# Layer norm woven between the y units, the last Q units behind the last convolution eviction, both halves of the out-projection behind the last y, the conv bias loaded early

## The chip, the core and the metric

The kernel runs on one core of a Trainium2 chip. The metric is the device time of one execution in microseconds. Five engines work from their own instruction queues, each in its own order: TensorE (PE in the profile, its weight loads PEld), VectorE (DVE), ScalarE (ACT), GpSimd (POOL) and SyncE (SP), which issues nearly all DMAs. An instruction waits for semaphores of other engines or DMAs; everything behind it on its engine waits with it.

## The reference

Two encoder layers on a sequence of 512 with 1024 channels, in f32. The change lies in the first layer's mixer:

```
z = h @ w_in                                   # 512 x 1536: za, zg, u
a = za * sigmoid(zg)
a = depthwise_conv(a, conv_w, width 31) + conv_b
ya = silu(layer_norm(a, ln_g, ln_b))           # 512 channels
y  = s5 forward + s5 backward + d * u          # 32 groups x 16 channels, 64 states
y  = gelu(y)
yb = y * sigmoid(y @ glu_w + glu_b)
h  = concat(ya, yb) @ w_out
x  = x + h
```

Behind it come the first feed-forward (SwiGLU, 2816 wide), the neighbourhood attention of the second layer and its feed-forward.

## The kernel before, in words

The order of the work is written out by hand: each engine does its instructions in the order in which the code emits them. Three things bend this order around the change.

*Background work.* `bgV` holds generators of small VectorE jobs. `tick(ns)` gives credit; jobs are emitted until their estimated costs have used it up, `charge(ns)` takes credit away, and `finish(job)` emits what is left of a job at once. The jobs here are the eight Q units, `job_q[i, hf]` (lines 969 to 977), each three VectorE instructions of 128 x 1024 (line 436: Q, wq, and Q plus wq), which make the operand of the y matmuls. Each of the 16 convolution steps gives `TCONV` of credit.

*Weights.* `W` streams 512 KB chunks: `load` issues the DMA on SyncE (line 73), `split` makes the high part `whi` on ScalarE (line 90) and the rest `wlo` on VectorE (line 92), and then loads the next chunk. `W.ahead()` splits up to two chunks ahead.

*PSUM.* Two rings of four banks, `psa` (convolution, mean, variance, cT, wo) and `psb` (y, yT, glu).

The stage goes like this. The convolution is four banks of four steps; each step is a set of small matmuls (line 993) against Toeplitz tables that ScalarE writes (line 761), one pair of steps' tables by VectorE (line 773). When a bank is full, VectorE adds the conv bias and writes it out (line 1003, into `an`) and sums it for the layer norm (line 1005, `lns`). The bias `cbB` comes by two DMAs on SyncE, behind the loads of the state-space tables `T`.

Then come four y units, `out_y(i, hq)`: each 4 groups of matmuls against T (line 1022) and Q (line 1025), and one eviction on ScalarE into `yn` (line 1028). `out_y(0, 0)` needs the Q units (0,0) and (2,0), `out_y(1, 1)` needs (1,1) and (3,1). The layer norm is in two parts: `ln_mean` (mean over channels by matmul, line 1064; two subtractions on VectorE, line 1068; eight squares with sums on ScalarE, line 1072) and `ln_scale` (variance by matmul, line 1077; a reciprocal root in twelve small VectorE instructions; scaling, line 1083 on VectorE, line 1081 on ScalarE). `out_a(ct)` transposes the normed rows back (cT, line 1090), applies silu (line 1102) and splits the result into `mah` and `mal`. `out_half(p, ...)` is one half of the out-projection of this branch: 24 matmuls of 128 x 512 (lines 200 to 202, tile `wo`). `out_t(ct)` transposes y (yT, line 1090; copy at line 1037), of which ct 0 and 2 need only the first two y units; `gelu` follows on both vector engines (lines 1043 to 1053) and then the GLU matmuls.

Of the kernel before, what the change touches and what calls it, by code (L numbers as in the profile page):

```python
# [19 lines left out]

CAP = 3000.0
HV = (4, 4)
TCONV = 2200
TCV = 10
QN, QT = 0, 2
LN, LT, LV = 1, 4, 6
# [4 lines left out]
P = 128  # L31
# [84 lines left out]
def tile_hybrid_encoder(ctx, tc, x, mix_norm, ffn_norm, ffn_w_gate, ffn_w_up, ffn_w_down,  # L116
# [4 lines left out]
    nc = tc.nc  # L121
# [48 lines left out]
    W = Weights(nc, wp, seq, NIN)  # L170
# [3 lines left out]
    def psa(name="psa"):  # L174
        return psp.tile([P, 512], F32, tag="a", name=name, bufs=4)

    def psb(name="psb"):
        return psp.tile([P, 512], F32, tag="b", name=name, bufs=4)
# [17 lines left out]
    def tmp(shape, tag, bufs=2, dt=F32):  # L196
        return sm.tile(shape, dt, tag=tag, name=tag, bufs=bufs)
# [76 lines left out]
    class Background:  # L274
# [20 lines left out]
        def tick(self, ns):  # L295
            self.credit = min(self.credit, CAP) + ns * self.share
            while self.credit > 0 and (self.jobs or self.fill):
                if self.jobs:
                    self.step()
                else:  # L300
                    self.step_fill()
# [16 lines left out]
    bgV = Background(1.0)  # L318
# [334 lines left out]
    for i in range(4):  # L653
# [19 lines left out]
        if i == 1:  # L673
# [4 lines left out]
            for t in range(4):  # L678
# [4 lines left out]
                         in_=ps[:, 64:64 + 4 * TAPS].rearrange("p (t j) -> p t j", t=4), func=AF.Copy)  # L683
# [3 lines left out]
            for t in range(LCH):  # L687
                p0 = 64 * (t % 2) + 16 * (t // 2)
                nc.sync.dma_start(out=wv[p0:p0 + 16],
                                  in_=bass.AP(tensor=wdb.tensor, offset=wdb.offset + t,  # L690
                                              ap=[[WPAD, 16], [16 * WPAD, G], [1, NLAG]]))
            A.activation(out=hgb, in_=col[:, R_GB:R_GB + 4], func=AF.Copy, scale=0.5)
        if i == 2:
            for r in range(2):
                ps = psb("ct")
                for t in range(4):
                    PE.transpose(out=ps[:, t * P:(t + 1) * P],
                                 in_=cnat[:, r, t].rearrange("p d n -> p (d n)"), identity=ident)
# [56 lines left out]
    def g_tc(n):  # L755

        t = slots[n // 2 % 3]
        for i in range(2):
            tcs[n + i] = t[:, :, i]
        for c in range(16):  # L760
            A.activation(out=t[:, :, :, c], in_=wvs[:, :, n:n + 2], func=AF.Copy, scale=mask16[:, c:c + 1])
            yield 1

    def make_tc(n):
        if n != TCV:
            for _ in g_tc(n):
                pass
            return
        t = slots[n // 2 % 3]
        for i in range(2):  # L770
            tcs[n + i] = t[:, :, i]
            for h in range(2):
                V.tensor_tensor(out=t[:, h, i], in0=wvs[:, h, n + i].unsqueeze(1).to_broadcast([P, 16, NLAG]),
                                in1=mask16.unsqueeze(2).to_broadcast([P, 16, NLAG]), op=ALU.mult)
        bgV.charge(3300)

    def g_tc_early():
        yield from g_tc(0)
        yield from g_tc(2)
# [51 lines left out]
    def scan_tables(i):  # L831
        e = phase[i]
        A.activation(out=e[:, 0], in_=e[:, 2], func=AF.Copy, scale=-1.0)
        A.activation(out=decays[:, i % 2, :, 1:], in_=m8[:, 1, 4 * i:4 * i + 4].unsqueeze(2).to_broadcast([P, 4, NCH - 1]),
                     func=AF.Copy)
# [59 lines left out]
    make_pb(3)  # L895
    scan_tables(0)
    tc_early = g_tc_early()
    f, b = slice(0, 64), slice(64, 128)
    for q in range(2):
        A.activation(out=pwQ[b, q].rearrange("p g t -> p t g"), in_=pw[b, q, 1:9], func=AF.Copy)  # L900
# [67 lines left out]
    def g_q(i, hf):  # L968
        yield from fused(Q[i][:, hf], wq, pwQ, 2 * i + hf, CT, CTs)


    cbB = tmp([P, 16, 16], "rstdB", 1)
    for h in range(2):
        src = conv_b[0, 256 * h:256 * h + 256]
        nc.sync.dma_start(out=cbB[64 * h:64 * h + 64],
                          in_=bass.AP(tensor=src.tensor, offset=src.offset, ap=[[0, 64], [1, 256]]))
    job_q = {(i, hf): g_q(i, hf) for i, hf in ((0, 0), (2, 0), (0, 1), (2, 1), (1, 0), (3, 0), (1, 1), (3, 1))}
    bgV.fill += job_q.values()
    for _ in tc_early:
# [6 lines left out]
    for b in range(4):  # L986
        ps = psa("conv")
        for gi in range(4):
            n = 4 * b + gi
            t = tcs.pop(n)  # L990
            for l in range(5):
                for h in range(2):
                    PE.matmul(out=ps[64 * h:64 * h + 64, gi * P:gi * P + P],
                              lhsT=AC[:, 16 * h + n, l:l + NCH],
                              rhs=t[:, h, :, 8 * l:8 * l + 8],
                              start=(l == 0), stop=(l == 4))
            if n % 2 and n + 5 < 16:
                make_tc(n + 5)
            tick(TCONV)
        if b == 2:  # L1000
            W.ahead()
        gs = slice(4 * b, 4 * b + 4)
        V.tensor_tensor(out=yc[:, :, gs], in0=ps.rearrange("p (g c t) -> p t g c", g=4, t=LCH),
                        in1=cbB[:, gs].unsqueeze(1).to_broadcast([P, LCH, 4, 16]), op=ALU.add)
        V.tensor_reduce(out=lns[:, b], in_=yc[:, :, gs].rearrange("p t g c -> p t (g c)"), axis=AX.X, op=ALU.add)
        bgV.charge(1200)
# [4 lines left out]
    def out_y(i, hq, between=None):  # L1011
        for key in ((i, hq), (i + 2, hq)):
            if key in job_q:
                bgV.finish(job_q[key])
        ps = psb("y")
        for gi in range(4):
            if gi == 2 and between is not None:
                between()
            gs = [h * 16 + i * 8 + hq * 4 + gi for h in range(2)]
            o = [ps[64 * h:64 * h + 64, gi * P:(gi + 1) * P] for h in range(2)]  # L1020
            for h, g in enumerate(gs):
                PE.matmul(out=o[h], lhsT=U[:, g], rhs=T[:, :, g], start=True, stop=False)
            for r in range(2):
                for h, g in enumerate(gs):
                    PE.matmul(out=o[h], lhsT=S2[:, r, g],
                              rhs=Q[g // 8][:, hq, r, gi].rearrange("p t c -> p (t c)"),
                              start=False, stop=(r == 1))
        A.activation(out=yn[:, :, i * 8 + hq * 4:i * 8 + hq * 4 + 4],
                     in_=ps.rearrange("p (g t c) -> p t g c", g=4, t=LCH), func=AF.Copy)
# [25 lines left out]
    def gelu(*cts):  # L1055
        for _ in g_lockstep(*(g_gelu(ct) for ct in cts)):
            pass
# [3 lines left out]
    def ln_mean():  # L1061
        ps = psa("mean")
        for b in range(4):
            PE.matmul(out=ps[:, 0:LCH], lhsT=pair, rhs=lns[:, b], start=(b == 0), stop=(b == 3))
        yv = yc.rearrange("p t g c -> p t (g c)")
        q = tmp([P, LCH], "lnq", 1)
        for t0 in (0, 4):
            V.tensor_tensor(out=yv[:, t0:t0 + 4], in0=yv[:, t0:t0 + 4],
                            in1=ps[:, t0:t0 + 4].unsqueeze(2).to_broadcast([P, 4, 256]), op=ALU.subtract)
            for t in range(t0, t0 + 4):  # L1070
                d = tmp([P, 256], "diag")
                A.activation(out=d, in_=yv[:, t], func=AF.Square, accum_out=q[:, t:t + 1])
        lnt["q"] = q

    def ln_scale():
        ps = psa("var")
        PE.matmul(out=ps[:, 0:LCH], lhsT=pair, rhs=lnt["q"], start=True, stop=True)
        r = rsqrt(ps[:, 0:LCH], LCH, 1e-5, 1.0)
        for t in range(LCH):
            if t in LNA:  # L1080
                A.activation(out=yc[:, t], in_=yc[:, t], func=AF.Copy, scale=r[:, t:t + 1])
            else:
                V.tensor_scalar(out=yc[:, t], in0=yc[:, t], scalar1=r[:, t:t + 1], scalar2=None, op0=ALU.mult)
# [9 lines left out]
    def mix_tile(n):  # L1093
        return lp.tile([P, 4, S], F32R, tag="Q", name=n, bufs=4)
# [11 lines left out]
    def out_a_low(ct):  # L1106
        V.tensor_tensor(out=mal[:, ct], in0=ya.pop(ct), in1=mah[:, ct].bitcast(F32), op=ALU.subtract)

    out_y(0, 0)
    bgV.finish(job_q[1, 0])  # L1110
    ln_mean()
    out_y(0, 1)
    out_y(1, 0)
    ln_scale()
    mah, mal = mix_tile("mah"), mix_tile("mal")
    for ct in range(4):
        out_a(ct)
    bgV.finish(job_q[1, 1])
    for ct in range(4):
        out_a_low(ct)  # L1120

# [2 lines left out]
    def out_half(p, mh, ml, first, ps_of=None):  # L1124
        wh, wl = W.next()
        W.ahead()
        for mi in range(2):
            m = 2 * p + mi
            if first:
                po[m] = ps_of("wo")  # L1130
            c = slice(mi * P, mi * P + P)
            for k in range(4):
                mm3(po[m], wh[:, k, c], wl[:, k, c], mh[:, k], ml[:, k], first and k == 0,
                    not first and k == 3)

    out_half(0, mah, mal, True, psa)
    out_y(1, 1)
    ygs = mp.tile([P, 2, 4, S], F32R, tag="S2", name="ygs")
    ygh, ygl = ygs[:, 0], ygs[:, 1]
    for ct in (0, 2, 1, 3):  # L1140
        out_t(ct)
    gelu(0, 2)
    gelu(1, 3)
    out_half(1, mah, mal, True, psa)
    mbh, mbl = mix_tile("mbh"), mix_tile("mbl")
# [68 lines left out]
    for m in range(KD):  # L1214
        ps = psa("dn")
        for a, b in ((0, 8), (8, 16), (16, 22)):
            wh, wl = W.next()
            W.ahead()
            for k in range(a, b):
# [20 lines left out]
                                          ap=[[465, 16], [-31, 8], [1, 248]]))  # L1240
# [145 lines left out]
    for n, cg in enumerate(QKV_ORDER):  # L1386
# [5 lines left out]
        for i in range(4):  # L1392
# [13 lines left out]
            for kk in range(2):  # L1406
                k = 2 * i + kk
                for j in range(4):
# [4 lines left out]
                    else:  # L1413
                        a, b = VSP[j - 1]
# [136 lines left out]
```

## Time and profile before

| | us |
|---|---|
| median of 3 runs | 1235.96 |
| runs | 1235.87 to 1237.0 |
| the profiled execution, device time | 1235.37 |
| its span in the trace | 1233.6 |
| TensorE matmul busy | 1198.1 (97%) |
| VectorE busy | 663.5 (54%) |
| ScalarE busy | 476.9 (39%) |
| GpSimd busy | 41.6 (3%) |
| TensorE busy from 150 to 200 us | 34.49 of 50 |

The table says that TensorE works nearly all the time. A share of the whole span hides the one stage that differs, from about 140 to 213 us: the end of the convolution, the y units, the layer norm, the out-projection's first part and the GELU. A timeline row of the section below gives the start, the length from the first instruction's start to the last one's end, the engine, the line of the kernel, the operation, the tiles written and read, the shapes and the count; in square brackets stands how long the engine had been idle before, and what released it. TensorE's clock has two levels, 1.2 and 2.4 GHz; the granted clock is the share of the higher one.

### The profile page before, as it was taken

The numbers are of one execution on the slowest core, as the hardware profiler recorded it, in microseconds if no ns is written. First come the engines' busy times: TensorE is split into PE (matmuls) and PEld (weight loads), VectorE is DVE, ScalarE is ACT, GpSimd is POOL, SyncE is SP. The second block draws the span as 40 slices with busy tenths as digits, with TensorE's granted clock in tenths as the row PEclk, the third lists the DMA queues.
The fourth block names the chain that finished last, engine by engine and source line by source line (L and its number), as shares of the span: only waits on it lengthen the run. The fifth ranks groups of instructions, "written<-read, shape, count | busy, mean of one in ns | idle before, by whom it ended". The sixth has DMA issues, their size and how long they took to land.

```text
span 1233.6 us, 16107 instructions
## 1 busy us (share of the span) xinstructions
PE 1198.1 (97%) x6427; PEld 951.3 (77%) x6427; DVE 663.5 (54%) x1110; ACT 476.9 (39%) x840; POOL 41.6 (3%) x90
## 2 busy tenths in 40 slices
PE   7999778999999999999999999999999999999998
PEld 4655566888888888888888887678888888888886
DVE  8899875664444444333337554856544444452322
ACT  5757756432232332222225465744323233222120
POOL 1100000000000000000000001520000000000000
PEclk9999978999999999999999999999999999999999
DMA  7411510333333323333354443303323333323331
GB/s 158 94 52 52 124 36 18 107 99 99 89 103 103 102 86 95 96 94 94 99 158 128 150 140 90 107 26 102 96 87 102 103 103 88 100 86 103 120 103 34
DMA packets 173154, 118.04 MB, mean 96 GB/s; under 512 B 21193, under 2 KB 153593, under 8 KB 173080
## 3 DMA queue, kind: packets, MB, share of 16 engines
q1 hardware_dynamic: 172616, 115.92, 32.4%
q10 hardware_dynamic: 400, 1.07, 0.4%
q8 instruction: 50, 0.82, 0.3%
q14 instruction: 24, 0.20, 0.0%
q0 software_dynamic: 64, 0.03, 0.0%
HBM read 109.04 MB, written 7.96 MB: 95 GB/s over the span
## 4 chain that ended last, share of the span: by engine, by line
PE 92%; DVE 3%; DMA 2%; SPq 2%; ACT 1%; issue 0%; DVEq 0%; POOL 0%; ACTq 0%; POOLq 0%
PE up L200 6%; PE gate L200 6%; PE gate L202 6%; PE up L202 6%; PE gate L201 6%; PE up L201 6%; PE qkv L1416 4%; PE qkv L1418 4%; PE qkv L1417 4%; PE dn L201 3%; PE dn L202 3%; PE dn L200 3%; PE dn L1517 3%; PE dn L1515 3%; PE dn L1516 3%; PE zg L730 2%
## 5 line engine op out<-in xcount | busy, mean ns | idle before, releaser
L92 DVE TENSOR_TENSOR wlo<-wraw,whi 128x1024 fp32r<-128x1024 f32 x176 | 213.0, 1213 | 256.0 <-ACT whi L90 254.7
L90 ACT ACTIVATE whi<-wraw 128x1024 fp32r<-128x1024 f32 x176 | 183.6, 1045 | 282.2 <-issue 113.9
L200 PE MATMUL gate<-xgh,whi 128*128 128x512 f32 x352 | 137.2, 390 | 0.0
L200 PE MATMUL up<-xgh,whi 128*128 128x512 f32 x352 | 137.1, 390 | 0.0
L202 PE MATMUL gate<-xgh,wlo 128*128 128x512 f32 x352 | 137.0, 389 | 0.0
L202 PE MATMUL up<-xgh,wlo 128*128 128x512 f32 x352 | 137.0, 389 | 0.0
L201 PE MATMUL gate<-xgl,whi 128*128 128x512 f32 x352 | 136.9, 389 | 0.0
L201 PE MATMUL up<-xgl,whi 128*128 128x512 f32 x352 | 136.9, 389 | 0.0
L1200 DVE TENSOR_TENSOR fu<-up,rstdB 128x512 f32<-128x512 f32 x44 | 30.4, 691 | 113.3 <-PE up L202 113.3
L1202 ACT ACTIVATE gh<-fu 128x512 fp32r<-128x512 f32 x44 | 27.8, 632 | 150.7 <-DVE fu L1201 150.7
L202 PEld LDWEIGHTS gate<-xgh,wlo 128*128 128x128 f32 x352 | 66.1, 188 | 13.8
L202 PEld LDWEIGHTS up<-xgh,wlo 128*128 128x128 f32 x352 | 66.0, 188 | 13.9
L201 PEld LDWEIGHTS gate<-xgl,whi 128*128 128x128 f32 x352 | 66.1, 188 | 13.7
L200 PEld LDWEIGHTS up<-xgh,whi 128*128 128x128 f32 x352 | 66.2, 188 | 13.6
L200 PEld LDWEIGHTS gate<-xgh,whi 128*128 128x128 f32 x352 | 66.0, 188 | 13.6
L201 PEld LDWEIGHTS up<-xgl,whi 128*128 128x128 f32 x352 | 66.0, 188 | 13.6
L200 PE MATMUL dn<-gh,whi 128*128 128x512 f32 x176 | 69.3, 394 | 0.0
L201 PE MATMUL dn<-gl,whi 128*128 128x512 f32 x176 | 69.3, 394 | 0.0
L202 PE MATMUL dn<-gh,wlo 128*128 128x512 f32 x176 | 69.3, 394 | 0.0
L1517 PE MATMUL dn<-whi,gl 128*128 128x512 f32 x176 | 69.2, 393 | 0.0
L1515 PE MATMUL dn<-whi,gh 128*128 128x512 f32 x176 | 69.0, 392 | 0.0
L1416 PE MATMUL qkv<-whi,xgh 128*128 128x512 f32 x176 | 68.8, 391 | 0.0
(298 smaller groups left out, 2017.0 us busy)
## 6 DMA issues: line engine op xcount, KB each, us to landing
wraw<-in_ffn_w_gate_dram SPq DMA_DIRECT2D x44, 512.0 KB
wraw<-in_ffn_w_up_dram SPq DMA_DIRECT2D x44, 512.0 KB
wraw<-in_ffn_w_down_dram SPq DMA_DIRECT2D x38, 512.0 KB
wraw<-in_na_w_qkv_dram SPq DMA_DIRECT2D x24, 512.0 KB
wraw<-in_ab_w_in_dram SPq DMA_DIRECT2D x12, 512.0 KB
bt<-bd SPq DMA_DIRECT2D x8, 640.0 KB
wraw<-in_ab_w_out_dram SPq DMA_DIRECT2D x8, 512.0 KB
wraw<-in_na_w_out_dram SPq DMA_DIRECT2D x8, 512.0 KB
```

What stands on the lines that cost most here:

```text
L90: self.nc.scalar.activation(out=hi, in_=raw, func=AF.Copy)
L92: eng.tensor_tensor(out=lo, in0=raw, in1=hi.bitcast(F32), op=ALU.subtract)
L200: PE.matmul(out=o, lhsT=lh, rhs=rh, start=start, stop=False)
L201: PE.matmul(out=o, lhsT=lh, rhs=rl, start=False, stop=False)
L202: PE.matmul(out=o, lhsT=ll, rhs=rh, start=False, stop=stop)
L1200: V.tensor_tensor(out=u, in0=pu, in1=rB, op=ALU.mult)
L1416: PE.matmul(out=pq[j], lhsT=lh, rhs=wh[:, kk], start=(k == 0), stop=False)
L1417: PE.matmul(out=pq[j], lhsT=lh, rhs=wl[:, kk], start=False, stop=False)
L1418: PE.matmul(out=pq[j], lhsT=ll, rhs=wh[:, kk], start=False, stop=(k == 7))
L1515: PE.matmul(out=pd[j], lhsT=gh[:, k, c], rhs=wh[:, kk], start=(k == 0), stop=False)
L1516: PE.matmul(out=pd[j], lhsT=gh[:, k, c], rhs=wl[:, kk], start=False, stop=False)
L1517: PE.matmul(out=pd[j], lhsT=gl[:, k, c], rhs=wh[:, kk], start=False, stop=(k == NF - 1))
```

## The change

`TCONV` goes from 2200 to 1750, so each convolution step emits less of the Q units. The bias DMAs move to the front of the state-space stage and `cbB` takes a buffer of the tag `diag`. `W.ahead()` moves from behind the third convolution bank to behind the layer norm's scaling. `ln_mean` is emitted between the second and third group of the first y unit, `ln_scale` behind the second y unit, `out_y(1, 1)` before the first half of the out-projection, and both halves stand behind the transposes of y, with half of the GELU emitted before each.

```
-TCONV = 2200
+TCONV = 1750
...
     tc_early = g_tc_early()
+    cbB = tmp([P, 16, 16], "diag")
+    for h in range(2):
+        src = conv_b[0, 256 * h:256 * h + 256]
+        nc.sync.dma_start(out=cbB[64 * h:64 * h + 64],
+                          in_=bass.AP(tensor=src.tensor, offset=src.offset, ap=[[0, 64], [1, 256]]))
...
-    cbB = tmp([P, 16, 16], "rstdB", 1)
-    for h in range(2):
-        src = conv_b[0, 256 * h:256 * h + 256]
-        nc.sync.dma_start(out=cbB[64 * h:64 * h + 64],
-                          in_=bass.AP(tensor=src.tensor, offset=src.offset, ap=[[0, 64], [1, 256]]))
...
             tick(TCONV)
-        if b == 2:
-            W.ahead()
...
-    out_y(0, 0)
-    bgV.finish(job_q[1, 0])
-    ln_mean()
+    out_y(0, 0, ln_mean)
+    for key in ((1, 0), (3, 0)):
+        bgV.finish(job_q[key])
     out_y(0, 1)
+    ln_scale()
+    for key in ((1, 1), (3, 1)):
+        bgV.finish(job_q[key])
+    W.ahead()
     out_y(1, 0)
-    ln_scale()
     mah, mal = mix_tile("mah"), mix_tile("mal")
     for ct in range(4):
         out_a(ct)
-    bgV.finish(job_q[1, 1])
+    out_y(1, 1)
     for ct in range(4):
         out_a_low(ct)
...
-    out_half(0, mah, mal, True, psa)
-    out_y(1, 1)
     ygs = mp.tile([P, 2, 4, S], F32R, tag="S2", name="ygs")
     ygh, ygl = ygs[:, 0], ygs[:, 1]
     for ct in (0, 2, 1, 3):
         out_t(ct)
     gelu(0, 2)
+    out_half(0, mah, mal, True, psa)
     gelu(1, 3)
     out_half(1, mah, mal, True, psa)
```

The instructions of every engine are the same in number; only their places differ. VectorE before, from the third bank's eviction to the layer norm (`an<-conv` is the eviction with the bias, `lns` its sum, `wlo` the weight splits, `an<-an,mean` the subtraction):

```order
L436 TENSOR_TENSOR Q<-pwQ,CT 128x1024
L92 TENSOR_TENSOR wlo<-wraw,whi 128x1024 x2
L1003 TENSOR_TENSOR an<-conv,rstdB 128x8x64
L1005 TENSOR_REDUCE lns<-an 128x8
L436 TENSOR_TENSOR wq<-pwQ,CTs 128x1024
L436 TENSOR_TENSOR Q<-Q,wq 128x1024
L1003 TENSOR_TENSOR an<-conv,rstdB 128x8x64
L1005 TENSOR_REDUCE lns<-an 128x8
L1068 TENSOR_TENSOR an<-an,mean 128x1024 x2
```

The same place on VectorE in the changed kernel:

```order
L1001 TENSOR_TENSOR an<-conv,diag 128x8x64
L1003 TENSOR_REDUCE lns<-an 128x8
L436 TENSOR_TENSOR Q<-Q,wq 128x1024
L436 TENSOR_TENSOR Q<-pwQ,CT 128x1024
L436 TENSOR_TENSOR wq<-pwQ,CTs 128x1024
L436 TENSOR_TENSOR Q<-Q,wq 128x1024
L436 TENSOR_TENSOR Q<-pwQ,CT 128x1024
L1001 TENSOR_TENSOR an<-conv,diag 128x8x64
L1003 TENSOR_REDUCE lns<-an 128x8
L1066 TENSOR_TENSOR an<-an,mean 128x1024 x2
```

Before, all Q instructions and two weight splits stand ahead of the last eviction. Now two Q instructions (wq and Q of the last unit) and the splits stand behind the scaling:

```order
L1081 TENSOR_SCALAR an<-an,rs_y 128x256 x5
L436 TENSOR_TENSOR wq<-pwQ,CTs 128x1024
L436 TENSOR_TENSOR Q<-Q,wq 128x1024
L92 TENSOR_TENSOR wlo<-wraw,whi 128x1024 x2
L1105 TENSOR_TENSOR mal<-sq,mah 128x512
```

ScalarE before, behind the convolution's tables (`diag,lnq<-an` are the squares, `yn` the y evictions, `sq<-cT` the first silu):

```order
L90 ACTIVATE whi<-wraw 128x1024 x2
L1028 ACTIVATE yn<-y 128x8x64
L1072 ACTIVATE diag,lnq<-an 128x256 x8
L1028 ACTIVATE yn<-y 128x8x64 x2
L1081 ACTIVATE an<-an,rs_y 128x256 x3
L1102 ACTIVATE sq<-cT,col 128x512
```

The same place on ScalarE in the changed kernel:

```order
L1070 ACTIVATE diag,lnq<-an 128x256 x8
L1026 ACTIVATE yn<-y 128x8x64 x2
L1079 ACTIVATE an<-an,rs_y 128x256 x3
L90 ACTIVATE whi<-wraw 128x1024 x2
L1026 ACTIVATE yn<-y 128x8x64
L1100 ACTIVATE sq<-cT,col 128x512
```

The weight copies move from ahead of the squares to behind the scaling, and the third y eviction behind them. On TensorE the mean stands between the second and third group of the first y unit, the variance between the second and third y unit, and the fourth y unit between the transposes cT and yT; the 24 matmuls of the first `out_half`, which stood right behind cT, stand behind yT.

## Rows read from the trace of the kernel before

**Rows 1.** Stages: busy us by engine (PE, PEld, DVE, ACT, POOL), granted clock, DMA.
```profile
150.00:200.00 50.00, 34.49 (x390) 31.02 (x388) 35.33 (x51) 28.14 (x76) 0.00 (x0) 0.80 0.10 30
```

**Rows 2.** Timeline of PE, 143 to 213 us: start, length, engine, line, tiles, count.
```profile
143.21 4.07 PE L993 MATMUL conv<-tcb,AC 128*64 128x128 f32 x40 [2.51 <-ACT tcb L761]
...
163.64 2.40 PE L993 MATMUL conv<-tca,AC 128*64 128x128 f32 x40 [1.78 <-ACT tca L761]
165.87 0.39 PE L1022 MATMUL y<-T,U 128*64 128x128 f32 x4
...
168.59 0.61 PE L1064 MATMUL mean<-lns,wpad 128*128 128x8 f32 x4
...
176.53 0.60 PE L1064 MATMUL mean<-lns,wpad 128*128 128x8 f32 x2 [3.12 <-DVE lns L1005]
...
184.34 0.39 PE L1077 MATMUL var<-lnq,wpad 128*128 128x8 f32 x2
...
188.80 3.28 PE L1090 MATMUL cT<-ident,an 64*128 64x64 f32 x32 [4.07 <-DVE an L1083]
...
202.40 1.78 PE L1090 MATMUL yT<-ident,yn 64*128 64x64 f32 x32
...
204.11 0.50 PE L200 MATMUL wo<-mah,whi 128*128 128x512 f32 x1
...
209.68 0.39 PE L200 MATMUL glu<-ygs,whi 128*128 128x512 f32 x1
...
212.54 0.50 PE L200 MATMUL glu<-ygs,whi 128*128 128x512 f32 x1 [1.34 <-ACT ygs L1051]
```

**Rows 3.** Timeline of DVE, 134 to 189 us.
```profile
134.30 1.23 DVE L436 TENSOR_TENSOR Q<-pwQ,CT 128x1024 f32<-128x1024 f32 x1
...
146.03 1.22 DVE L436 TENSOR_TENSOR wq<-pwQ,CTs 128x1024 f32<-128x1024 f32 x1
150.63 0.69 DVE L1003 TENSOR_TENSOR an<-conv,rstdB 128x512 f32<-128x512 f32 x1 [3.38 <-DMA rstdB<-in_conv_b_dram]
...
153.09 3.03 DVE L773 TENSOR_TENSOR tcb<-wv,mask 128x640 f32<-128x640 f32 x4
...
175.07 0.68 DVE L1003 TENSOR_TENSOR an<-conv,rstdB 128x512 f32<-128x512 f32 x1
...
177.16 2.35 DVE L1068 TENSOR_TENSOR an<-an,mean 128x1024 f32<-128x1024 f32 x2 [0.69 <-PE mean L1064]
...
187.25 1.40 DVE L1083 TENSOR_SCALAR an<-an,rs_y 128x256 f32<-128x256 f32 x5
```

**Rows 4.** Timeline of ACT, 163 to 206 us.
```profile
163.49 2.00 ACT L90 ACTIVATE whi<-wraw 128x1024 fp32r<-128x1024 f32 x2
...
178.42 0.42 ACT L1072 ACTIVATE diag<-an 128x256 f32<-128x256 f32 x1 [9.11 <-DVE an L1068]
...
181.84 0.60 ACT L1028 ACTIVATE yn<-y 128x512 f32<-128x512 f32 x1
...
189.92 0.78 ACT L1102 ACTIVATE sq<-cT,col 128x512 f32<-128x512 f32 x1 [1.44 <-PE cT L1090]
...
194.77 0.63 ACT L1104 ACTIVATE mah<-sqacc 128x512 fp32r<-128x512 f32 x1
...
203.14 2.07 ACT L1037 ACTIVATE AC<-yT 128x512 f32<-128x512 f32 x4
```

**Rows 5.** Timeline of SP (DMA issues), 40 to 75 and 140 us.
```profile
40.78 5.81 SPq L73 DMA_DIRECT2D wraw<-in_ab_w_in_dram  x2
...
63.18 10.64 SPq L73 DMA_DIRECT2D wraw<-in_ab_w_in_dram  x2
...
140.00 1.19 SPq L975 DMA_DIRECT2D rstdB<-in_conv_b_dram  x2
```

**Rows 6.** Slices of 2 us; columns as in rows 1, clock behind POOL.
```profile
192.00:194.00 2.00, 2.00 (x6) 1.57 (x6) 0.83 (x2) 1.94 (x5) 0.00 (x0) 0.50 0.00 0
194.00:196.00 2.00, 1.96 (x7) 1.02 (x5) 1.26 (x2) 1.97 (x4) 0.00 (x0) 0.85 0.00 0
```

## The prediction

> **What bounds the kernel now.** The stage table comes first: nearly everywhere TensorE is busy without a break, but between 150 and 200 us it has work for 34.49 of 50 us, at a mean granted clock of 0.80 [rows 1]. This is the stage that the change touches, so I read it engine by engine in the timeline, and only there.
>
> TensorE [rows 2]: the last convolution matmuls end at 163.64 + 2.40 = 166.04, and what holds them back is ScalarE, which writes their tables until 163.49 [rows 4]. Four groups of y follow at once, until 168.59. Then TensorE waits for the row sums of the last two convolution banks, until 176.53; it does eight groups of y and the variance by 184.34 + 0.39, waits 4.07 for the scaled rows until 188.80, does one half of the out-projection, the last y, the transposes yT, the second half, and reaches the GLU at 209.68, where one more wait of 1.34 ends at 212.54.
>
> VectorE [rows 3] is the reason for the wait until 176.53. It works through the Q units, one instruction each 1.173 us ((146.03 - 134.30) / 10). It stands still for 3.38 us until the conv bias lands at 150.63, and evicts the last bank at 175.07, nine microseconds after that bank was complete. So the chain here is: bias and Q instructions ahead of the eviction, then mean, squares, variance, scaling, transposes, out-projection. ScalarE is the second thread [rows 4]: squares from 178.42, silu and copies 189.92 to 194.77 + 0.63.
>
> **The change part by part.** I follow the new order through the rows' durations.
>
> *Bias early.* Its two issues move on SyncE from 140.0 to behind the loads at 40.78; the queue issues nothing between 46.59 and the next load, at 63.18 [rows 5], so they fill a gap, and the only thing behind them there is a load that has nearly 17 us of slack. The 3.38 us wait goes. Without that cover the two issues would push the weight loads back by 1.19 us, what they took at 140.00.
>
> *TCONV and the Q units.* Ten Q instructions now stand before the first eviction, where eleven stood: it starts at 134.30 + 10 x 1.173 = 146.03, when its bank has long been full. Eviction and reduction, 0.69 each, end at 147.41. The four table instructions need the buffer that TensorE leaves at 143.21 + 4.07 = 147.28 and take 3.03: 150.44. Two Q instructions: 152.79. Second eviction: 154.17. Five Q: 160.04; third eviction: 161.42; five Q: 167.29. The fourth eviction waits only for that, since its bank is full at 166.04. Before, 1.46 us lay between its start and the mean on TensorE (175.07 to 176.53), so the mean comes at 168.75 instead of 176.53. Two Q instructions and the two weight splits are left over; they come after the scaling.
>
> *Layer norm between the y units.* TensorE does two groups of y (0.68 each by 165.87 to 168.59), waits at the mean for about 1.5 us with the rest of y behind it, and has then six groups, 4.1 us, until about 173.4. The first subtraction starts 0.63 after the mean (169.38), the squares 1.26 after that (170.64), and eight of them take 3.42 (178.42 to the y eviction at 181.84): 174.06. So the variance waits for ScalarE, not for y, and runs at 174.1 instead of 184.34. ScalarE has nothing else to do there, for the weight copies that stood at 163.49 have been moved.
>
> From the variance to the transposes cT took 4.46 (184.34 to 188.80): 178.56 now. The next y unit, 2.7 us, lies inside it. VectorE ends the scaling 4.31 after the variance (187.25 + 1.40), 178.41, and the two left Q instructions at 180.76, before TensorE wants them: cT takes 3.28 at the lower clock, or what yT took, 1.78, at the higher one, and ends between 180.3 and 181.8.
>
> *What is late next* is ScalarE. After its scaling (about 178.4) it has the two weight copies (2.00: 180.4), a y eviction (0.60: 181.0), four silu and four copies (189.92 to 195.40, 5.48: 186.5) and the last y eviction (187.1). The last y needs 2.72 to 5.4 us from cT's end, so TensorE gets there first, does the two yT that do not need this eviction, and waits until 187.1 for the other two. Half of yT's 1.78 and TensorE is at 188.0, where both halves of the out-projection now stand in a row, 5.57 each by 204.11 to 209.68: GLU at 199.1.
>
> *GELU.* Before, 9.40 us lay between the first copy of yT (203.14) and the GLU matmul that waits for it (212.54). From 187.1 and with the weight split between the two halves (1.0 to 2.2 us more) this is 197.5 to 198.7, before TensorE is there; the wait of 1.34 goes too. What comes in its place is out-projection that fills the same time.
>
> *The clock.* In the profile a wait of 1.78 us left the higher clock as it was (40 convolution matmuls in 2.40 after it; at the lower one 40 took 4.07). After the wait of 3.12 the eight y groups took 184.34 - 176.53 - 0.60 (the mean) = 7.21 instead of 5.44, and after that of 4.07 the granted clock was 0.50, which is 1.2 GHz, until about 194.6 (0.85 in the slice from 194 to 196) [rows 2, 6]. The new wait at the mean, 1.5, is like the first; the one at yT, some 2.6, nearer to 3.12 than to 1.78. So I charge what the 3.12 cost, 1.8 us, to the out-projection: GLU at 200.9. Bounds of this cost: nothing, or 2.9, half of the 5.8 us during which the clock stayed low after 188.80. A fall at the mean would cost at most the six y groups at half speed, which puts the variance at 177.5: 3.4 more.
> [...]
>
> *Sum.* The GLU matmul of 212.54 comes at 200.9 + 1.4 (six matmuls of 5.57 / 24) = 202.3, 10.2 us earlier. GLU and everything behind it keep their order and their work, and TensorE has no wait of note there. The profiled execution took 1235.37 (span 1233.6), so **1225.2 us**. The median shown, 1235.96, is 0.6 above that execution, which the range has to take in. The sum's own ends: without a low clock and with the fourth eviction at 166.1 (1.2 earlier), 10.2 + 1.8 + 1.2 = 13.2 less, 1222.2; with both clock bounds against it, 12.0 - 3.4 - 2.9 = 5.7 less, 1229.7.
>
> **The rivals.**
> *The clock falls at every wait.* Then y loses its 1.8 us after the mean, of which 0.7 is hidden behind the squares, and the rest is as above: 1226.3. For it: two of the three waits quoted. Against it: the third, and that the new one at the mean is the shortest. [...]
>
> *TensorE does not get its clock back at all.* The stretch is all short instructions, transposes and small matmuls, and after 188.80 the clock stayed at 0.50 through cT and into the out-projection [rows 6]. If 0.50 holds from the mean to the GLU, y, cT, y, yT and 48 out-projection matmuls run at half speed: variance 177.5, cT at 182.9 (behind y, 5.4), 186.2, y 191.6, yT 3.56, 195.2, out-projection 22.3, 217.5, against 211.2 for a GLU without its wait: 6.3 later, 1241.7, slower than before. It turns the sign once more than 12 us of full-speed work run at half speed. Against it: in each burst shown the higher clock came back within six microseconds, and the out-projection is dense.
>
> *The weave does not move the mean.* If another VectorE or ScalarE wait that the new order makes (the table instructions for their buffer, or ScalarE's tables) kept the fourth eviction near 175, the variance would still follow the mean by 5.3 instead of 7.8, and the out-projection and the GLU wait would still save something: 7.78 of the 10.2 gone, 1233.0. Against it: ScalarE's tables are the same instructions in the same order.
>
> *Given back later.* If the weight loads, whose issue is tied to the splits that move back by up to 11 us, came too late for the FFN, the gain would be a wait there: 1235.4, no change. Against it: the loads for the second GLU half and the chunk behind it go out at about 182, and TensorE wants them after 200.
>
> **Numbers.** The forecast with its bounds 0.80; clock at every wait 0.08; mean not moved 0.04; given back 0.04; clock lost 0.04. A measurement of this kernel tells 0.2%, 2.5 us, from no change. Faster than 1233.5 are the first three, less a little: 0.92; within: 0.04; slower: 0.04. The range 1221.8 to 1230.0 holds the first two, with the lower end a little below the sum's own and the 0.6 of the median above it.
>
> **What will show it.** No wait for the conv bias on VectorE, the last eviction at 167 to 168 right behind a Q instruction. The mean near 168.8, the variance waiting for ScalarE's squares near 174. cT near 178.5. One TensorE wait of 2 to 3 us before the last two yT, released by ScalarE's last y eviction near 187, then 48 out-projection matmuls without a gap, and a GLU without a wait. The forecast is wrong if the last eviction still comes after 170, if the out-projection begins after 191, or if the FFN shows TensorE waits that were not there.

## The result, and the profile after

The changed kernel takes 1224.5 us (median of 4 runs, 1223.91 to 1224.9), the kernel before 1236.48 beside it (1235.87 to 1237.51): a ratio of 0.9902, 95% interval 0.9887 to 0.9916, some 12 us. The forecast was 1225.2 with the range 1221.8 to 1230.0. The profiled execution took 1224.9, with a span of 1223.1. Against the profiled execution of before, 1235.37, that is 10.5 us; that execution lies 1.1 below the median of its kernel, so the medians are further apart than the two traces.

The stage table, in the columns of [rows 1]: TensorE works 41.48 of these 50 us where it had 34.49, and the mean clock is 0.91 instead of 0.80.

```profile
150.00:200.00 50.00, 41.48 (x501) 37.14 (x498) 41.58 (x61) 38.58 (x95) 0.00 (x0) 0.91 0.10 33
```

TensorE's timeline, in the columns of [rows 2]:

```profile
164.03 2.40 PE L993 MATMUL conv<-tca,AC 128*64 128x128 f32 x40 [2.70 <-ACT tca L761]
...
168.78 0.39 PE L1062 MATMUL mean<-lns,wpad 128*128 128x8 f32 x2 [0.28 <-DVE lns L1003]
...
173.82 0.39 PE L1075 MATMUL var<-lnq,wpad 128*128 128x8 f32 x2 [0.57 <-ACT diag L1070]
...
178.29 1.98 PE L1088 MATMUL cT<-ident,an 64*128 64x64 f32 x32 [1.31 <-DVE an L1081]
...
183.14 1.01 PE L1088 MATMUL yT<-ident,yn 64*128 64x64 f32 x16
186.25 1.60 PE L1088 MATMUL yT<-ident,yn 64*128 64x64 f32 x16 [2.10 <-ACT yn L1026]
187.78 0.79 PE L200 MATMUL wo<-mah,whi 128*128 128x512 f32 x1
...
201.29 0.39 PE L200 MATMUL glu<-ygs,whi 128*128 128x512 f32 x1
...
202.65 0.39 PE L200 MATMUL glu<-ygs,whi 128*128 128x512 f32 x1
```

The convolution ends at 166.43, as before but for 0.39 by which this whole trace runs later at that point. From there on every row comes earlier than its like: the mean at 168.78 (176.53 in [rows 2]), the variance at 173.82 (184.34), cT at 178.29 (188.80), the GLU at 201.29 (209.68), and its seventh matmul at 202.65 without a wait (212.54). The waits in between have shrunk to 0.28, 0.57 and 1.31; the new one is 2.10, before the last two yT.

VectorE, in the columns of [rows 3], and the bias loads on SyncE:

```profile
146.42 0.68 DVE L1001 TENSOR_TENSOR an<-conv,diag 128x512 f32<-128x512 f32 x1
...
167.32 0.68 DVE L1001 TENSOR_TENSOR an<-conv,diag 128x512 f32<-128x512 f32 x1
...
176.74 1.40 DVE L1081 TENSOR_SCALAR an<-an,rs_y 128x256 f32<-128x256 f32 x5
...
179.31 1.23 DVE L436 TENSOR_TENSOR Q<-Q,wq 128x1024 f32<-128x1024 f32 x1
```
```profile
47.03 1.13 SPq L901 DMA_DIRECT2D diag<-in_conv_b_dram  x2
```

No wait stands before the first eviction, and the last one comes at 167.32 instead of 175.07. Of the two left-over Q instructions, both behind the scaling, the last ends at 180.54, where TensorE has just left cT.

ScalarE, in the columns of [rows 4], and three 2 us slices in those of [rows 6]:

```profile
177.88 1.99 ACT L90 ACTIVATE whi<-wraw 128x1024 fp32r<-128x1024 f32 x2
179.78 0.57 ACT L1026 ACTIVATE yn<-y 128x512 f32<-128x512 f32 x1
180.25 0.76 ACT L1100 ACTIVATE sq<-cT,col 128x512 f32<-128x512 f32 x1
...
185.62 0.58 ACT L1026 ACTIVATE yn<-y 128x512 f32<-128x512 f32 x1
```
```profile
186.00:188.00 2.00, 1.75 (x17) 1.63 (x18) 0.44 (x1) 1.77 (x5) 0.00 (x0) 0.57 0.30 105
...
190.00:192.00 2.00, 2.00 (x6) 1.53 (x5) 1.82 (x4) 1.85 (x4) 0.00 (x0) 0.50 0.00 0
...
194.00:196.00 2.00, 2.00 (x10) 1.65 (x9) 1.90 (x4) 1.15 (x3) 0.00 (x0) 1.00 0.07 23
```

ScalarE runs without a break from the scaling to the last y eviction at 185.62, and TensorE's wait of 2.10 ends with that eviction. The granted clock, 1.00 from 168 to 186, is 0.50, 1.2 GHz, behind that wait until about 193.

### The profile page after: what moved, and what is told of

It reads as the page before. It is cut to its first block, busy times and chain, and to the rows that moved or that the text cites. A ratio compares the mean times of both kernels' runs of the same rounds, so it can differ in the third digit from the quotient of the medians.

```text
span 1223.1 us, 16107 instructions
## 1 busy us (share of the span) xinstructions
PE 1193.8 (98%) x6427; PEld 947.2 (77%) x6427; DVE 663.5 (54%) x1110; ACT 476.4 (39%) x840; POOL 41.3 (3%) x90
## 4 chain that ended last, share of the span: by engine, by line
PE 84%; ACT 1%; DVE 0%; issue 0%; POOL 0%; POOLq 0%; DVEq 0%
PE up L200 7%; PE gate L201 7%; PE up L201 7%; PE gate L200 7%; PE gate L202 7%; PE up L202 7%; PE qkv L1416 4%; PE qkv L1417 4%; PE qkv L1418 4%; PE dn L200 3%; PE dn L202 3%; PE dn L201 3%; PE dn L1517 3%; PE dn L1515 3%; PE dn L1516 3%; PE wo L200 3%
## 5 line engine op out<-in xcount | busy, mean ns | idle before, releaser
L201 PEld LDWEIGHTS up<-xgl,whi 128*128 128x128 f32 x352 | 66.0, 187 | 13.5
```

The lines of the kernel that those rows point to most:

```text
L201: PE.matmul(out=o, lhsT=lh, rhs=rl, start=False, stop=False)
```

## The experiments

The question was which part of the change gives the 12 us, and what the wait that is left costs. Each kernel was timed beside the kernel before (1235.8 to 1236.2 us in these comparisons); ratios are to it. An interval leaves each ratio open by one to two us either way. "More" or "less than the changed kernel" is the difference of the two medians, which come from different comparisons; differences as small as 1.6 or 2.2 us therefore rest on the traces more than on the times.

**Bias early, nothing else** (in the kernel before; the two DMAs move with the tile):

```
     tc_early = g_tc_early()
+    cbB = tmp([P, 16, 16], "diag")
...
-    cbB = tmp([P, 16, 16], "rstdB", 1)
     job_q = {(i, hf): g_q(i, hf) for i, hf in ((0, 0), (2, 0), (0, 1), (2, 1), (1, 0), (3, 0), (1, 1), (3, 1))}
```

> Only the bias loads move to the front; TCONV, W.ahead and the order of the tail are as before. Theory A (VectorE's queue sets the mean): the 3.38 us wait on VectorE goes, every later eviction comes 3.4 us sooner, the last at 171.7 instead of 175.07 and the mean at 173.1, and all behind it follows: 3.4 us less than the kernel before. Rival B (the tail's order sets the time and an earlier mean only makes another wait longer): under 1 us less.

1232.51 us, ratio 0.9964 (0.9951 to 0.9977): 3.5 us less. VectorE:

```profile
171.66 0.68 DVE L1003 TENSOR_TENSOR an<-conv,diag 128x512 f32<-128x512 f32 x1
```

The last eviction moved from 175.07 to 171.66, by the 3.4 us of the wait for the bias [rows 3], and the program by as much. Rival B is out.

**The front alone.** Bias early, TCONV and W.ahead as in the change, but the tail in the order of before:

```
-TCONV = 2200
+TCONV = 1750
...
-        if b == 2:
-            W.ahead()
...
     out_y(1, 0)
     ln_scale()
+    W.ahead()
```

> Bias early, TCONV 1750 and W.ahead behind the layer norm's scaling, but the tail in the order of before (variance behind the third y unit, first half of the out-projection behind cT, last y and yT behind it). Theory A: mean at 168.8 as in the changed kernel; eight y groups then end near 174.8 and the variance comes there, cT 179.2, first half from about 183 with a wait for the low parts until 186.4, done near 189, last y to 191.7, yT, first copy of yT near 192.4, GLU held up by GELU until about 201.8, where the changed kernel has 202.65: 10 to 11 us less than before, within 1 us of the changed kernel. Rival B: the weave of the tail carries most of the gain, so this one saves no more than 5 us.

1233.45 us, ratio 0.9978 (0.9969 to 0.9987): 2.6 us less, where 10 to 11 were expected. By its number this is Theory A's failure, but the trace (of an execution of 1235.42 us, 2 above the median) shows a fault of the kernel's own order. TensorE's wait (in total, times, longest) and VectorE's timeline:

```profile
PE y L1023 <- DVE Q L436: 4.0, 1, 4.0
```
```profile
191.91 1.22 DVE L92 TENSOR_TENSOR wlo<-wraw,whi 128x1024 fp32r<-128x1024 f32 x1 [4.78 <-ACT whi L90]
193.05 1.22 DVE L436 TENSOR_TENSOR wq<-pwQ,CTs 128x1024 f32<-128x1024 f32 x1
```

The two left-over Q instructions were emitted with the last y, so they stood behind a weight split (191.91) whose ScalarE half waited for the first half of the out-projection. The last y waited 4.0 us for them, and the clock fell in that wait (0.50 from about 195 to 201). The second attempt puts them where the change has them:

```
     ln_scale()
+    for key in ((1, 1), (3, 1)):
+        bgV.finish(job_q[key])
     W.ahead()
```

> As e2_front, but the two left-over Q instructions stand behind the scaling, ahead of the weight splits, as in the changed kernel (in e2_front they stood behind a split that waited for TensorE, and the last y waited 3.99 us for them). Theory A': front and tail are worth about 8 and 5 us apart and overlap: cT still waits 4.1 us behind the variance and runs at the lower clock, first half 182.7 to 190.9, last y to 193.6, first copy of yT near 194.8, GLU held by GELU until 204.2: 8 us less than before, 3 to 4 more than the changed kernel. Rival B' (the tail carries the gain): 5 us or less, like e2_front.

1229.54 us, ratio 0.9940 (0.9927 to 0.9953): 6.7 us less. Theory A' expected 8 less and holds in kind; B' is out.

```profile
PE cT L1088 <- DVE an L1081: 4.1, 1, 4.1
...
PE glu L200 <- ACT ygs L1049: 1.3, 1, 1.3
PE wo L201 <- DVE mal L1105: 1.2, 1, 1.2
```

The mean is as early as in the changed kernel, and what remains are waits of the old tail: 4.1 us for the scaled rows, 1.3 for GELU, and one of 1.2 for the low parts, since the out-projection now catches up with them. Behind the wait for GELU the granted clock fell, which it did not do there in the kernel before:

```profile
208.00:210.00 2.00, 2.00 (x6) 1.51 (x6) 1.83 (x3) 0.83 (x2) 0.00 (x0) 0.50 0.35 75
```

From the seventh GLU matmul to the end this trace takes 1.7 us longer than the trace of before (1022.8 against 1021.1), so some of what is missing from the expected 8 was lost to the clock there.

**The tail alone.** The new order of y units, layer norm and out-projection; bias, TCONV and W.ahead as before (the diff is to the changed kernel; the call of `W.ahead()` behind the scaling stays, and no split is left for it):

```
-    cbB = tmp([P, 16, 16], "diag")
+    cbB = tmp([P, 16, 16], "rstdB", 1)
...
-TCONV = 1750
+TCONV = 2200
...
+        if b == 2:
+            W.ahead()
```

> The tail in the new order, but bias late, TCONV 2200 and W.ahead at the third bank as before. Theory A: mean stays at 176.5, variance behind the squares at 181.9 instead of 184.34, cT 186.3, last y eviction near 193.6, out-projection from 194.6, GLU near 207.6 without its wait, against an effective 211.2: 3 to 4 us less than before. Rival B: 8 us or more less.

1230.72 us, ratio 0.9958 (0.9945 to 0.9972): 5.3 us less, between the two expectations and nearer to Theory A.

```profile
PE mean L1064 <- DVE lns L1005: 8.0, 2, 4.9
...
PE cT L1090 <- DVE an L1083: 1.3, 1, 1.3
PE yT L1090 <- ACT yn L1028: 1.0, 1, 1.0
```

The wait for the row sums is 8.0, more than before, and the waits for the scaled rows and GELU are down to 1.3 and nothing. Front 6.7 and tail 5.3 add up to the 12.0 of the whole change by the medians, each good to about 1.6 us by its interval; Theory A' had them at about 8 and 5 and overlapping. That the shares simply add is not shown: by the spans of the traces they are 5.5 and 3.1, against 10.5 for the whole, and each of the two kernels lost some 1.6 us to a fall of the clock of its own, the front in the GLU and the tail in the out-projection (48 matmuls in 12.6 us, granted clock 0.59 and 0.56 in the slices from 196 to 200). What is shown is that neither part gives the whole.

**One part of the change undone at a time.** First TCONV, back at 2200:

> The changed kernel with TCONV back at 2200. All Q instructions then stand before the last eviction, two more than in the changed kernel. Theory A (every VectorE instruction ahead of the last eviction delays the whole chain): last eviction at 169.7 instead of 167.3, all behind it 2.3 us later: 1226.8. Rival G (two Q instructions are hidden, since they would otherwise stand behind the scaling): within 0.6 us of 1224.5.

1226.69 us, ratio 0.9919 (0.9906 to 0.9932), 2.2 more than the changed kernel, as Theory A said. Its four executions lie from 1225.1 to 1228.1, so the time alone does not exclude G; the trace speaks against it. VectorE's last eviction:

```profile
169.13 0.69 DVE L1001 TENSOR_TENSOR an<-conv,diag 128x512 f32<-128x512 f32 x1
```

It comes 1.8 us later than in the changed kernel, and 2.4, two Q instructions, counted from the first of them, which starts 0.6 earlier in this trace. The mean is 1.8 later (170.59) and the GLU 2.8 (204.11), after one more fall of the clock, among the y units.

Then the bias loads, back behind T:

> The changed kernel with the bias loads left where they were, behind the loads of T. Theory A (every delay of VectorE's queue ahead of the last eviction goes through to the end): VectorE reaches the first eviction at 146.4 and waits until the bias lands near 150.6, 4.2 us; last eviction 171.5, mean near 173, all behind it 4.2 us later: 1228.7. Rival H (the wait is made up for, since the table instructions and later evictions have slack): within 1 us of 1224.5.

1227.63 us, ratio 0.9937 (0.9924 to 0.9951), 3.1 more, where 4.2 were expected (4.3 by the two ratios, so the times do not tell 3.1 from 4.2). TensorE, then VectorE:

```profile
173.40 0.60 PE L1062 MATMUL mean<-lns,wpad 128*128 128x8 f32 x2 [5.31 <-DVE lns L1003]
...
192.17 1.02 PE L1088 MATMUL yT<-ident,yn 64*128 64x64 f32 x16 [2.10 <-ACT yn L1026]
193.12 0.50 PE L200 MATMUL wo<-mah,whi 128*128 128x512 f32 x1
...
204.15 0.39 PE L200 MATMUL glu<-ygs,whi 128*128 128x512 f32 x1
```
```profile
151.05 0.69 DVE L1001 TENSOR_TENSOR an<-conv,rstdB 128x512 f32<-128x512 f32 x1 [4.96 <-DMA rstdB<-in_conv_b_dram]
```

The wait for the bias is 4.96, the mean comes 4.6 later than in the changed kernel and the out-projection 5.3 later, but the GLU only 2.9 later: 48 matmuls take 11.0 us here and 13.5 there. The clock fell in the longer wait at the mean (0.50 from about 171 to 177), so the first y groups behind it ran at 1.2 GHz and put the variance off by 1.3 more; it had risen again before the out-projection. The wait of 2.10 before the last two yT is the same as in the changed kernel, released by the same eviction, and here the granted clock stays at 1.00 behind it. And W.ahead back at the third bank:

```
             tick(TCONV)
+        if b == 2:
+            W.ahead()
```

> The changed kernel with W.ahead at the third bank as before (two Q instructions more are then left for behind the scaling, by the charge). Theory A: the two splits on VectorE wait for ScalarE's weight copies, which stand behind the last tables at 163.9, so the third eviction comes near 167.4 and the last near 172.3, 5 us later than in the changed kernel, and so does the out-projection: 1229 to 1230. Rival I (ScalarE is the bound behind the variance, and taking its 2 us of copies out of that chain pays for the later mean): 1225 to 1227.

1227.71 us, ratio 0.9935 (0.9923 to 0.9946), 3.2 more (4.1 by the two ratios); Theory A expected 5, rival I at most 2.5. VectorE, then TensorE:

```profile
165.22 2.36 DVE L92 TENSOR_TENSOR wlo<-wraw,whi 128x1024 fp32r<-128x1024 f32 x2 [4.66 <-ACT whi L90]
...
172.22 0.69 DVE L1003 TENSOR_TENSOR an<-conv,diag 128x512 f32<-128x512 f32 x1
```
```profile
188.91 0.54 PE L1025 MATMUL y<-Q,S 128*64 128x128 f32 x5 [2.01 <-DVE Q L436]
```

The place and the 4.66 us wait for ScalarE's copies are as Theory A had them; the mean is 4.9 later and the GLU 2.9, for the reason seen in the kernel before this one (out-projection again 11.0 us, at the higher clock). This edit moves more than the splits: four Q instructions instead of two stand behind the scaling, and the last y waits 2.01 for them, in place of the wait of 2.10 before the last two yT, which is gone.

**What the wait before the last two yT costs.** Three kernels, all from the changed one. The first moves the first half of the out-projection into the wait:

```
-    for ct in (0, 2, 1, 3):
+    for ct in (0, 2):
         out_t(ct)
     gelu(0, 2)
     out_half(0, mah, mal, True, psa)
+    for ct in (1, 3):
+        out_t(ct)
     gelu(1, 3)
```

> The changed kernel, with the first half of the out-projection put between the two yT that do not need the last y eviction and the two that do. Theory A (the wait for ScalarE's last y eviction, 2.10 us, and the low clock behind it are all that TensorE still loses there): out-projection from 184.2, the higher clock held, the last two yT near 190, GLU's seventh matmul near 197.9 instead of 202.65: 4 to 5 us less than the changed kernel, 1219.5 to 1220.5. Rival B (the GELU chain or the low parts of the first half hold TensorE up anyway): within 2 us of the changed kernel.

1220.17 us (1219.55 to 1220.44), ratio 0.9868 (0.9853 to 0.9883), 4.3 less than the changed kernel, as Theory A said. TensorE:

```profile
183.71 1.02 PE L1088 MATMUL yT<-ident,yn 64*128 64x64 f32 x16
184.66 0.50 PE L200 MATMUL wo<-mah,whi 128*128 128x512 f32 x1
...
190.32 1.02 PE L1088 MATMUL yT<-ident,yn 64*128 64x64 f32 x16
...
196.86 0.39 PE L200 MATMUL glu<-ygs,whi 128*128 128x512 f32 x1
```

TensorE does not wait any more, and the first half takes 5.66 us, at the higher clock. (In this execution the clock had fallen and risen again during cT and the last y groups, 0.50 from 179 to 182, much as in the third kernel below.) The second puts the last y eviction on VectorE:

```
...
+        if (i, hq) == (1, 1):
+            V.tensor_copy(out=ov, in_=iv)
+        else:
+            A.activation(out=ov, in_=iv, func=AF.Copy)
```

> The changed kernel with the last y eviction on VectorE instead of behind silu and copies on ScalarE. Theory E (ScalarE's queue is what TensorE waits for before the last two yT): eviction at 183.3 to 184.0, yT from 184, out-projection from about 185 with small waits for the low parts, higher clock held, GLU near 196.5: 4 to 5 us less than the changed kernel, 1219.5 to 1220.5. Rival F (the GELU chain or the low parts take the place of the wait): 2 us or less.

1219.28 us (1218.84 to 1219.44), ratio 0.9859 (0.9846 to 0.9872), 5.2 less than the changed kernel: Theory E, a little better. It is the fastest kernel of this study.

```profile
182.39 1.93 PE L1091 MATMUL yT<-ident,yn 64*128 64x64 f32 x32
184.26 0.50 PE L200 MATMUL wo<-mah,whi 128*128 128x512 f32 x1
...
195.28 0.39 PE L200 MATMUL glu<-ygs,whi 128*128 128x512 f32 x1
```
```profile
182.50 0.69 DVE L1028 COPY yn<-y 128x512 f32<-128x512 f32 x1 [0.44 <-PE y L1023]
```

All 32 transposes run in one piece while VectorE copies; the low parts and GELU do not hold TensorE up, and the granted clock stays at 1.00 where it fell in the two others:

```profile
180.00:182.00 2.00, 2.00 (x40) 2.00 (x39) 2.00 (x2) 1.89 (x4) 0.00 (x0) 1.00 0.06 12
```

The third fills the wait with work that is thrown away, eight matmuls into a bank that the first real one overwrites:

```
     for ct in (0, 2):
         out_t(ct)
+    fill = psa("wo")
+    for _ in range(8):
+        PE.matmul(out=fill, lhsT=W.hl[W.pos][0][:, 0, 0:P], rhs=mah[:, 0], start=True, stop=True)
...
-    out_half(0, mah, mal, True, psa)
+    out_half(0, mah, mal, True, lambda n: psa(n) if 0 in po else fill)
```

> The changed kernel with eight extra out-projection matmuls (128 x 512, their sum is overwritten by the first real one) in TensorE's 2.10 us wait before the last two yT. Theory C (the wait before yT is what takes the clock down behind it): no wait of note there, the granted clock stays at 1.00, both halves take 11 us instead of 13.5 and yT 1.0 instead of 1.6: 3 us less than the changed kernel, 1221.5, though it does 1.8 us of work more. Rival D (the clock falls for another reason, such as the transposes before it): within 0.6 us of 1224.5.

1222.9 us (1221.9 to 1223.16), ratio 0.9887 (0.9874 to 0.9900), 1.6 less than the changed kernel, half of what Theory C said. TensorE, and a slice before:

```profile
185.03 2.11 PE L1143 MATMUL wo<-mah,whi 128*128 128x512 f32 x8
187.08 1.02 PE L1088 MATMUL yT<-ident,yn 64*128 64x64 f32 x16
188.03 0.50 PE L200 MATMUL wo<-mah,whi 128*128 128x512 f32 x1
...
199.04 0.39 PE L200 MATMUL glu<-ygs,whi 128*128 128x512 f32 x1
```
```profile
180.00:182.00 2.00, 2.00 (x23) 2.00 (x21) 2.00 (x2) 1.89 (x4) 0.00 (x0) 0.50 0.05 12
```

With the wait filled, yT takes 1.0 and the two halves 11.0 us, at a granted clock of 1.00, as C has it. But in this execution the clock had already fallen once behind cT (0.50 from 180 to 182), which cost the last y some 1.5 us. So behind a filled wait the clock stays up; whether it would have fallen there anyway, having just risen, this run does not settle. In the kernel with the late bias it stayed up behind the same wait unfilled (192.17 above), so the wait is not by itself what takes it down, and what does stays open.

## Why the prediction was right

Its steps, in the order in which it made them, in us of the trace:

| step | predicted | measured |
|---|---|---|
| first eviction | 146.03 | 146.42 |
| last eviction | 167.29 | 167.32 |
| mean | 168.75 | 168.78 |
| variance | 174.1 | 173.82 |
| cT | 178.56 | 178.29 |
| end of the last y eviction | 187.1 | 186.20 |
| wait before the last two yT | 2.6 | 2.10 |
| out-projection begins | 188.0 | 187.78 |
| extra time at the lower clock | 1.8 | 2.5, and 0.6 in yT |
| GLU | 200.9 | 201.29 |
| execution | 1225.2 | 1224.9 |

The trace of the changed kernel runs 0.39 later than that of before already at the first Q instruction, so differences of that size in the table mean nothing: the first eviction's is this shift alone, and the last eviction's 0.03 hides that VectorE's chain was 0.36 shorter than predicted.

The bound was named rightly: VectorE's queue ahead of the last eviction. The three kernels with one part undone, and the early bias alone, show that an instruction or a wait added there delays the mean, and that the end follows in whole or for the greater part: the medians differ by 3.5, 2.2, 3.1 and 3.2 where the mean differs by 3.4, 1.8, 4.6 and 4.9. So was what is late next, ScalarE's queue behind the variance: taking the last y eviction out of it was worth 5.2 us.

Mis-sized, in both directions: ScalarE's chain was 0.9 too long, since the instruction behind its scaling began at 177.88 instead of 178.4 and instructions behind one another overlap (the y eviction of 179.78 is followed 0.47 later, not 0.60); and the low clock cost 3.1 rather than 1.8: the 48 matmuls of the out-projection took 13.5 (187.78 to 201.29) instead of the 11.0 of the kernels in which it stayed up, and half of yT 1.60 instead of 1.01. The two nearly cancel, which is luck, and so is part of the nearness of the time: 10.2 us less were forecast, the medians give 12.0 and the traces 10.5. The wait at the mean was put at 1.5 and was 0.28 by the trace, since the six mean matmuls of the first three banks, whose sums were there, run in the meantime (0.83 us from 167.67); nothing followed from that. The 2.6 for the wait at yT is not worked out in the prediction; its own terms give 1.7 to 3.1, by the two ends of cT. And the upper end of the range, 1230.0, leaves 0.3 above the sum's 1229.7, not the 0.6 that it names.

The 1.8 was taken from a row that was read wrongly. The slow y groups behind the wait of 3.12 were put down to that wait, but in the trace of before the clock had fallen earlier, at about 171, in a wait of 3.61 that [rows 2] do not show, and had not risen since:

```profile
172.81 0.59 PE L1064 MATMUL mean<-lns,wpad 128*128 128x8 f32 x2 [3.61 <-DVE lns L1005]
```
```profile
172.00:174.00 2.00, 0.59 (x2) 0.50 (x2) 1.93 (x4) 0.00 (x0) 0.00 (x0) 0.50 0.89 274
```

So the 3.12 does not price a wait of that length. A row of before that does is the one at 143.21 [rows 2]: a wait of 2.51, and 40 matmuls in 4.07 instead of 2.40 behind it, 1.7 more. That the clock would fall behind the new wait at yT came true in the changed kernel, but the kernel with the late bias has the same wait without a fall: what makes the clock fall there is not shown, and this term came out in part by luck.

Of the rivals, "the weave does not move the mean" is refuted by the last eviction at 167.32, and "TensorE does not get its clock back" by the out-projection's second half at 1.00. "Given back later" is refuted too: from 215 us on TensorE's longest wait in either trace is 0.2 us. "The clock falls at every wait" did not happen: behind the waits at the mean, the variance and cT it stayed up. The Trainium skill, page "TensorE: Matmul & The Clock Gate", section "HAM oscillation — how this bites in real kernels", tells of a kernel whose bursts of matmuls are each shorter than the wait behind them, and of which every one starts again at the lower clock. No run here shows that case: between the four waits of this trace (0.28, 0.57, 1.31 and 2.10) TensorE works for 3 to 6 us at a time, longer than any of them, and the clock fell behind the last alone.

The reading of the shares written before the experiments, that the front would give nearly all and the tail's own gain would be swallowed, was wrong: the front alone gave 6.7, the tail alone 5.3. Which piece of the tail gives its share was not tested.

## What to carry to other kernels

Where an engine's queue is written by hand, the instruction to look at is the one that another engine waits for, and what stands ahead of it: here two background instructions (2.2 us), two weight splits with their wait for ScalarE's copies (3.2) and a late 128 KB load (3.1 to 3.5) each showed at the end of a program whose main engine was 97% busy. When such a chain has been shortened, ask at once which queue is last now, and put independent work of the waiting engine into that gap: moving one block of 24 matmuls by 16 transposes was worth another 4.3 us.

## What was not expected of the hardware

The length of a wait alone does not tell whether TensorE's clock falls behind it. In the changed kernel a wait of 2.70 before the convolution matmuls at 148.71 was followed by 40 of them in 4.06 us, one of 2.70 before those at 164.03 by 40 in 2.40 (shown above), and one of 2.10 before yT by a granted clock of 0.50. In the kernel with the late bias the same wait of 2.10 before the same yT was followed by a clock of 1.00, and in the tail alone one of 1.04 there by a clock of 0.59 (196 to 198).

```profile
148.71 4.06 PE L993 MATMUL conv<-tca,AC 128*64 128x128 f32 x40 [2.70 <-ACT tca L761]
```

Where it falls also decides what it costs: the kernels with the later mean paid for it among the y units and then ran the out-projection 2.5 us faster, so their GLU came 2.9 later where their mean came 4.6 and 4.9 later.
